# TensorE's program as a loop of four-row steps, and x in front of W: a LoRA linear layer on one core

## The chip, the core and the metric

The kernel runs on one core of a Trainium2 chip. The core has five engines that run side by side, each with a program of its own: TensorE (PE in the profile, with its weight loads as PEld), VectorE (DVE), ScalarE (ACT), GpSimd (POOL) and SyncE (SP, which here only issues transfers). Sixteen DMA engines move data between the chip's main memory and the on-chip memory SBUF, which has 128 partitions. TensorE writes its results to another memory, PSUM, and VectorE and ScalarE take them out of there. Engines wait for one another by semaphores.

The metric is the device time of one execution in microseconds (us); lower is better.

## What is computed

```python
# x (16, 2048, 256), W (256, 256), lora_A (256, 16), lora_B (16, 256), lora_E (16,), scale = 1.0
x_flat = x.reshape(-1, 256)                       # 32768 rows
y = x_flat @ W
lora_out = ((x_flat @ lora_A) * lora_E) @ lora_B
return (y + scale * lora_out).reshape(16, 2048, 256)
```

All inputs and the output are float32. x and the output have 33.55 MB each.

## The kernel before

The small matrices are folded first: `weff = W + scale * (lora_A * lora_E) @ lora_B`, once, in bf16 (lines 88 to 105: a cast, two transposes, a scaling, two matmuls and an addition). After that the whole work is `x_flat @ weff`.

The 32768 rows of x are cut into nine chunks (`PLAN`): 16 rows a partition, then seven times 32, then 16 again, times 128 partitions. A chunk is one load of 2 or 4 MB (`load`, line 66) into one of six slots of SBUF, and one store of the same size (`store`, line 70) out of the same slot, since the result is written over x in place. All loads and stores, and W ahead of them (line 73), are issued by SP and stand in one queue. SP issues W, then the loads of the first four chunks (`LEAD`); after that, whenever a chunk is done, its store and then the load of the chunk four places on. A load into a slot that was used before waits until the store out of it has landed. ScalarE issues the loads of lora_A, lora_B and lora_E.

A chunk is worked off in groups of two rows a partition (`CG`). For a group TensorE makes four transposes of 128x128 (two rows, two halves of the 256 columns) straight from the f32 data of x, into PSUM (`transposed`, line 113). VectorE casts the 128x512 result to bf16 and puts it in SBUF (line 119). TensorE multiplies the four pieces with weff, two summed into each of two rows (line 131). ScalarE copies the 128x512 result from PSUM over x (line 139).

The order of the work is that of the code. In TensorE's program the transposes of group n+1 stand in front of the products of group n, so that it has work while VectorE casts. At the end of a chunk, the products of the chunk's last group therefore stand behind the first transposes of the next chunk, and so behind that chunk's landing. Everything is written out: there is no loop on any engine, and TensorE's program has some 2,070 instructions, 16 for each of the 128 groups and a few for the small matrices.

Of the kernel before, what the change touches and what calls it, by code (L numbers as in the profile page):

```python
# [1 line left out]

# [5 lines left out]

PLAN = [16] + [32] * 7 + [16]

ROWS, SLOTS = 32, 6

LEAD = 4
CG = 2


@with_exitstack
def kernel(  # L20
    ctx: ExitStack,
    tc: tile.TileContext,
    x: bass.AP,
    W: bass.AP,
    lora_A: bass.AP,
    lora_B: bass.AP,
    lora_E: bass.AP,
    scale: bass.AP,
    out: bass.AP,
):  # L30
    nc = tc.nc
    P = 128
    FP32 = mybir.dt.float32
    BF16 = mybir.dt.bfloat16

    x_flat = x.flatten_outer_dims()
    out_flat = out.flatten_outer_dims()
    N, K = x_flat.shape
    M = out_flat.shape[1]
    R = lora_B.shape[0]  # L40
    KC = K // P
    assert K == M and sum(PLAN) * P == N

    const = ctx.enter_context(tc.tile_pool(name="const", bufs=1))
    slots = ctx.enter_context(tc.tile_pool(name="slots", bufs=SLOTS))
    xTpool = ctx.enter_context(tc.tile_pool(name="xTpool", bufs=4))
    ps_setup = ctx.enter_context(tc.tile_pool(name="ps_setup", bufs=1, space=bass.MemoryType.PSUM))
    ps_xT = ctx.enter_context(tc.tile_pool(name="ps_xT", bufs=3, space=bass.MemoryType.PSUM))
    ps_y = ctx.enter_context(tc.tile_pool(name="ps_y", bufs=3, space=bass.MemoryType.PSUM))


    ctx.enter_context(tc.manual_schedule())

    starts = [sum(PLAN[:i]) * P for i in range(len(PLAN))]

    def rows_of(flat, i):
        b, r0 = PLAN[i], starts[i]
        return flat[r0:r0 + b * P, :].rearrange("(p b) k -> p b k", b=b)

    held = []

    def load(i):
        t = slots.tile([P, ROWS, K], FP32, name="xy")
        nc.sync.dma_start(out=t[:, :PLAN[i], :], in_=rows_of(x_flat, i))  # L66
        held.append(t)

    def store(i):
        nc.sync.dma_start(out=rows_of(out_flat, i), in_=held[i][:, :PLAN[i], :])  # L70

    w_sb = const.tile([P, KC, M], FP32)
    nc.sync.dma_start(out=w_sb, in_=W.rearrange("(c p) m -> p c m", p=P))  # L73
    a_sb = const.tile([P, KC, R], FP32)
    nc.scalar.dma_start(out=a_sb, in_=lora_A.rearrange("(c p) r -> p c r", p=P))
    b_sb = const.tile([R, M], FP32)
    nc.scalar.dma_start(out=b_sb, in_=lora_B)
    e_sb = const.tile([R, 1], FP32)
    nc.scalar.dma_start(out=e_sb, in_=lora_E[:, None])

    for i in range(LEAD):
        load(i)

    ident = const.tile([P, P], FP32)
    make_identity(nc, ident)

    b_bf = const.tile([R, M], BF16)
    nc.vector.tensor_copy(out=b_bf, in_=b_sb)  # L88
    ps_at = ps_setup.tile([R, KC, P], FP32, name="ps_at")
    for c in range(KC):  # L90
        nc.tensor.transpose(ps_at[:, c, :], a_sb[:, c, :], ident)  # L91
    ate = const.tile([R, KC, P], BF16)
    nc.vector.tensor_scalar(  # L93
        out=ate,
        in0=ps_at,
        scalar1=e_sb,
        scalar2=float(scale),
        op0=mybir.AluOpType.mult,
        op1=mybir.AluOpType.mult,
    )  # L100
    ps_aeb = ps_setup.tile([P, KC, M], FP32, name="ps_aeb")
    for c in range(KC):
        nc.tensor.matmul(ps_aeb[:, c, :], ate[:, c, :], b_bf, start=True, stop=True)  # L103
    weff = const.tile([P, KC, M], BF16)
    nc.vector.tensor_add(out=weff, in0=w_sb, in1=ps_aeb)  # L105

    groups = [(i, g) for i, b in enumerate(PLAN) for g in range(b // CG)]

    def transposed(i, g):
        psum_xt = ps_xT.tile([P, CG, KC, P], FP32, name="psum_xt")  # L110
        for j in range(CG):
            for c in range(KC):
                nc.tensor.transpose(  # L113
                    psum_xt[:, j, c, :],
                    held[i][:, g * CG + j, c * P:(c + 1) * P],
                    ident,
                )
        xt = xTpool.tile([P, CG, KC, P], BF16, name="xt")
        nc.vector.tensor_copy(out=xt, in_=psum_xt)  # L119
        return xt  # L120


    ready = transposed(*groups[0])
    for n, (i, g) in enumerate(groups):
        xt = ready
        if n + 1 < len(groups):
            ready = transposed(*groups[n + 1])
        psum_y = ps_y.tile([P, CG, M], FP32, name="psum_y")
        for j in range(CG):
            for c in range(KC):  # L130
                nc.tensor.matmul(  # L131
                    psum_y[:, j, :],
                    xt[:, j, c, :],
                    weff[:, c, :],
                    start=(c == 0),
                    stop=(c == KC - 1),
                )

        nc.scalar.copy(out=held[i][:, g * CG:(g + 1) * CG, :], in_=psum_y)  # L139
        if (g + 1) * CG == PLAN[i]:  # L140
            store(i)
            if i + LEAD < len(PLAN):
                load(i + LEAD)


# [1 line left out]
_INS = ['x', 'W', 'lora_A', 'lora_B', 'lora_E', 'scale']  # L147
_OUTS = [((16, 2048, 256), 'float32')]

_NUMBERS = {'scale': 1.0}  # L150


# [26 lines left out]
```

## Time and profile before

| | us |
|---|---|
| median of three runs | 166.19 (165.45, 166.19, 166.29) |
| the profiled execution | 166.25 |
| its span, first to last instruction | 164.4 |
| PE busy | 123.3 (75% of the span) |
| DVE busy | 90.0 (55%) |
| ACT busy | 76.3 (46%) |
| POOL busy | 0.7 (0%) |
| DMA, data of x, W and out (queue q1) | 96.2% of 16 engines |

The page divides the span into 40 slices of 4.1 us and gives for each, in tenths, the share of time in which an engine was busy; for the DMA engines it is the mean over the sixteen, and GB/s is what they moved. The part on queues gives packets, MB and the share of sixteen engines' time. A row of the groups of instructions names the line, the engine, the operation, what it writes and reads with shapes, how often; then busy time and the mean of one in ns; then the idle time of the engine in front of it, and what ended it. The chain that ended last is followed back from the end of the program: at each step to what released it. SPq is SP's queue of issues. PEclk, the clock that TensorE was granted, is full for most of the span, with some slower stretches (one near 96 us), and half after the last matmul.

The transposes start at 9.68 us, when the first chunk has landed, and the last copy of ScalarE ends at 138.7. TensorE waited for loads of x four times, 6.0 us in all.

### The profile page before, as it was taken

The page shows a single profiled execution, that of the slowest core. Times are in us where ns is not written, and L with a number is a line of the kernel's source. Part 1 is how long each engine was busy: PE and PEld are TensorE (multiplying, and loading weights), DVE is VectorE, ACT ScalarE, POOL GpSimd, SP SyncE. Part 2 cuts the span into 40 slices and gives each one's busy share as a digit, 9 for nine tenths or more (in the row PEclk, how much of TensorE's full clock was granted, in tenths as well). Part 3 has the DMA queues.
Part 4 walks back from the last instruction along what each step waited for, and adds up shares of the span by engine and source line. Part 5 has one row for each costly group of instructions (what it writes and reads, how often), then busy time and mean ns, then how long its engine had stood idle before and what let it go on. Part 6 is the DMA issues. An engine that isn't in the chain of part 4 may idle for free.

```text
span 164.4 us, 2548 instructions
## 1 busy us (share of the span) xinstructions
PE 123.3 (75%) x1028; PEld 102.9 (63%) x1028; DVE 90.0 (55%) x131; ACT 76.3 (46%) x129; POOL 0.7 (0%) x6
## 2 busy tenths in 40 slices
PE   0179899999999999999999689992999995000000
PEld 0058788888888888888888478881888783000000
DVE  0065677777777777777777536771777673000000
ACT  0034566666666666666666525662566565000000
POOL 1000000000000000000000000000000000000000
PEclk9999999999999999999999978999999999655555
DMA  5999999998999999999999999999999999999991
GB/s 141 429 482 407 415 478 395 454 415 343 437 462 407 421 446 431 435 431 423 439 419 439 423 423 443 409 439 447 423 391 466 415 443 423 423 454 415 415 391 56
DMA packets 3211, 67.56 MB, mean 411 GB/s; under 512 B 624, under 2 KB 896, under 8 KB 896
## 3 DMA queue, kind: packets, MB, share of 16 engines
q1 hardware_dynamic: 2864, 67.37, 96.2%
q8 instruction: 8, 0.13, 0.3%
q10 hardware_dynamic: 336, 0.03, 0.2%
q14 instruction: 3, 0.02, 0.0%
HBM read 33.85 MB, written 33.55 MB: 410 GB/s over the span
## 4 chain that ended last, share of the span: by engine, by line
DMA 59%; PE 23%; ACT 1%; SPq 1%; DVE 0%; issue 0%
DMA xy<-in_x_dram 38%; DMA out_dram<-xy 21%; PE psum_y L131 12%; PE psum_xt L113 11%; ACT xy L139 1%; DVE xt L119 0%; SPq L66 0%; SPq L73 0%
## 5 line engine op out<-in xcount | busy, mean ns | idle before, releaser
L119 DVE CAST xt<-psum_xt 128x512 bf16<-128x512 f32 x128 | 88.5, 691 | 38.6 <-PE psum_xt L113 38.6
L139 ACT COPY xy<-psum_y 128x512 f32<-128x512 f32 x128 | 75.0, 586 | 52.7 <-PE psum_y L131 52.7
L113 PE MATMUL psum_xt<-ident,xy 128*128 128x128 f32 x512 | 79.2, 279 | 6.1 <-DMA xy<-in_x_dram 6.0
L131 PE MATMUL psum_y<-weff,xt 128*128 128x256 bf16 x512 | 79.3, 278 | 0.3 <-DVE xt L119 0.3
L113 PEld LDWEIGHTS psum_xt<-ident,xy 128*128 128x128 f32 x512 | 61.9, 144 | 9.2 <-issue 5.7
L131 PEld LDWEIGHTS <-xt 128*128 128x128 bf16 x512 | 41.1, 99 | 16.8 <-DVE xt L119 0.9
L139 ACT ACT_TABLE_LOAD x1 | 1.3, 1283 | 9.7 <-DMA xy<-in_x_dram 9.7
L103 PE MATMUL ps_aeb<-b_bf,ate 16*128 16x256 bf16 x2 | 0.6, 402 | 4.4 <-DVE ate L93 4.4
L91 PE MATMUL ps_at<-ident,a_sb 128*16 128x128 f32 x2 | 0.6, 396 | 4.0 <-DMA a_sb<-in_lora_A_dram 4.0
L88 DVE CAST b_bf<-b_sb 16x256 bf16<-16x256 f32 x1 | 0.3, 281 | 6.0 <-DMA b_sb<-in_lora_B_dram 6.0
L103 PEld LDWEIGHTS <-ate 16*128 16x128 bf16 x2 | 0.1, 102 | 4.9 <-DVE ate L93 4.9
L91 PEld LDWEIGHTS ps_at<-ident,a_sb 128*16 128x16 f32 x2 | 0.1, 88 | 4.0 <-issue 4.0
L93 DVE TENSOR_SCALAR ate<-ps_at,e_sb 16x256 bf16<-16x256 f32 x1 | 0.5, 472 | 2.2 <-DMA e_sb<-in_lora_E_dram 2.2
L105 DVE TENSOR_TENSOR weff<-w_sb,ps_aeb 128x512 bf16<-128x512 f32 x1 | 0.7, 689 | 0.7 <-PE ps_aeb L103 0.7
masks.py:199 POOL TENSOR_SCALAR_AFFINE_SELECT ident<-ident 128x128 f32<-128x128 f32 x1 | 0.3, 292 | 0.1
masks.py:197 POOL MEMSET ident<- 128x128 f32 x1 | 0.2, 204 | 0.3 <-POOLq L160 0.3
L160 POOL MEMSET const-bfloat16-1.0<- 128x1 bf16 x1 | 0.1, 101 | 0.0
L160 POOL MEMSET const-uint8-127<- 128x1 uint8 x1 | 0.1, 101 | 0.0
L160 POOL MEMSET const-float32-0.0<- 128x1 f32 x1 | 0.1, 98 | 0.2 <-issue 0.2
L160 POOL MEMSET const-float32-1.0<- 128x1 f32 x1 | 0.1, 98 | 0.0
## 6 DMA issues: line engine op xcount, KB each, us to landing
xy<-in_x_dram SPq DMA_DIRECT2D x7, 4096.0 KB, 38.0
out_dram<-xy SPq DMA_DIRECT2D x7, 4096.0 KB, 34.2
xy<-in_x_dram SPq DMA_DIRECT2D x2, 2048.0 KB, 26.6
out_dram<-xy SPq DMA_DIRECT2D x2, 2048.0 KB, 24.5
w_sb<-in_W_dram SPq DMA_DIRECT2D x1, 256.0 KB, 3.0
a_sb<-in_lora_A_dram ACTq DMA_DIRECT2D x1, 16.0 KB, 3.2
b_sb<-in_lora_B_dram ACTq DMA_DIRECT2D x1, 16.0 KB, 4.7
e_sb<-in_lora_E_dram ACTq DMA_DIRECT2D x1, 0.1 KB, 6.6
```

The source lines that it names most:

```text
L88: nc.vector.tensor_copy(out=b_bf, in_=b_sb)
L91: nc.tensor.transpose(ps_at[:, c, :], a_sb[:, c, :], ident)
L93: nc.vector.tensor_scalar(out=ate, in0=ps_at, scalar1=e_sb, scalar2=float(scale), op0=mybir.AluOpType.mult, op1=mybir.AluOpType.mult,)
L103: nc.tensor.matmul(ps_aeb[:, c, :], ate[:, c, :], b_bf, start=True, stop=True)
L105: nc.vector.tensor_add(out=weff, in0=w_sb, in1=ps_aeb)
L113: nc.tensor.transpose(psum_xt[:, j, c, :], held[i][:, g * CG + j, c * P:(c + 1) * P], ident,)
L119: nc.vector.tensor_copy(out=xt, in_=psum_xt)
L131: nc.tensor.matmul(psum_y[:, j, :], xt[:, j, c, :], weff[:, c, :], start=(c == 0), stop=(c == KC - 1),)
L139: nc.scalar.copy(out=held[i][:, g * CG:(g + 1) * CG, :], in_=psum_y)
L160: nc = _bacc.Bacc("TRN2", target_bir_lowering=False, num_devices=1)
```

## The change

The kernel is written anew with semaphores of its own, inside one critical section in which each engine's program is written out by hand. The chunks, the slots, the lead of four loads and the folding of the small matrices stay. What differs:

- SP issues the load of the first chunk, then W, then the three other loads. Afterwards the order is that of before: wait for a chunk, store, load (with the wait for the slot's old store in front of the load).
- A step has four rows a partition instead of two (`Q`). VectorE first casts the step's x from SBUF to a bf16 buffer (`round_step`, 128x1024); there are two such buffers, used in turn. TensorE transposes from there with a bf16 identity, eight transposes a step into bf16 PSUM. VectorE casts 128x1024 from PSUM to one of two `xt` buffers. Eight products go to one of two `ps_y`, and ScalarE copies 128x1024 over x.
- VectorE's order is: cast of x for step k+1, then the copy out of PSUM for step k. weff, which needs W, stands in front of the first cast of x.
- Since the buffers of TensorE are the same every second step, its program is a loop of 31 passes of two steps (transposes 1, products 0, transposes 0, products 1), with the first transposes ahead of it and the last step and a half behind it. In the loop it can't wait for growing counts, so each wait takes one off its semaphore (`take`). Per step it takes from the cast of x, from the copy out of PSUM, and from ScalarE's copy.
- ScalarE drains after the last copy of a chunk and then tells SP.

TensorE's program shrinks to 32 matmuls inside the loop and 36 outside. VectorE executes 128 casts as before, 64 of each kind, each of 1024 elements a partition; ScalarE 64 copies of 1024 elements instead of 128 of 512.

```diff
-    for i in range(LEAD):
-        load(i)
...
-    def transposed(i, g):
-        psum_xt = ps_xT.tile([P, CG, KC, P], FP32, name="psum_xt")
...
-        nc.vector.tensor_copy(out=xt, in_=psum_xt)
...
+    xb = [sbuf(f"xb{s}", [P, Q, K], BF16) for s in range(2)]
+    xt = [sbuf(f"xt{s}", [P, Q, KC, P], BF16) for s in range(2)]
...
+    ps_xt = [psum(f"ps_xt{s}", [P, Q, KC, P], BF16) for s in range(2)]
+    ps_y = [psum(f"ps_y{s}", [P, Q, M], FP32) for s in range(2)]
...
+    with tc.tile_critical(sync_engine=mybir.EngineType.SP, no_gpsimd_drain=True):
...
+        def load(i):
+            sp.dma_start(out=xy[i % SLOTS][:, :PLAN[i], :], in_=rows_of(x_flat, i)).then_inc(s_in[i], 16)
+
+        for i in range(LEAD):
+            load(i)
+            if i == 0:
+                sp.dma_start(out=w_sb[:], in_=W.rearrange("(c p) m -> p c m", p=P)).then_inc(s_w, 16)
+        for i in range(CHUNKS):
+            sp.wait_ge(s_rdy, i + 1)
+            sp.dma_start(out=rows_of(out_flat, i), in_=xy[i % SLOTS][:, :PLAN[i], :]).then_inc(s_out[i], 16)
+            if i + LEAD < CHUNKS:
+                if i + LEAD >= SLOTS:
+                    sp.wait_ge(s_out[i + LEAD - SLOTS], 16)
+                load(i + LEAD)
+        for i in range(CHUNKS):
+            sp.wait_ge(s_out[i], 16)
...
+        dve.wait_ge(s_w, 16)
+        dve.wait_ge(s_lpe, 2)
+        dve.tensor_add(out=weff[:], in0=w_sb[:], in1=ps_aeb[:]).then_inc(s_lora, 1)
+
+        def round_step(k):
+            i, r = steps[k]
+            if r == 0:
+                dve.wait_ge(s_in[i], 16)
+            if k >= 2:
+                dve.wait_ge(s_t, k - 1)
+            dve.tensor_copy(out=xb[k % 2][:], in_=xy[i % SLOTS][:, r:r + Q, :]).then_inc(s_xb, 1)
+
+        round_step(0)
+        for k in range(n):
+            if k + 1 < n:
+                round_step(k + 1)
+            dve.wait_ge(s_t, k + 1)
+            if k >= 2:
+                dve.wait_ge(s_p, k - 1)
+            dve.tensor_copy(out=xt[k % 2][:], in_=ps_xt[k % 2][:]).then_inc(s_xt, 1)
...
+        for k, (i, r) in enumerate(steps):
+            act.wait_ge(s_p, k + 1)
+            act.copy(out=xy[i % SLOTS][:, r:r + Q, :], in_=ps_y[k % 2][:]).then_inc(s_y, 1)
+            if r + Q == PLAN[i]:
+                act.drain().then_inc(s_rdy, 1)
...
+        def take(s):
+            pe.wait_ge(s, 1).then_inc(s, -1)
+
+        def transposes(k):
+            take(s_xb)
+            for j in range(Q):
+                for c in range(KC):
+                    t = pe.transpose(ps_xt[k % 2][:, j, c, :], xb[k % 2][:, j, c * P:(c + 1) * P], ident_bf[:])
+            t.then_inc(s_t, 1)
+
+        def products(k):
+            take(s_xt)
+            take(s_y)
+            for j in range(Q):
+                for c in range(KC):
+                    m = pe.matmul(
+                        ps_y[k % 2][:, j, :], xt[k % 2][:, j, c, :], weff[:, c, :],
+                        start=(c == 0), stop=(c == KC - 1),
+                    )
+            m.then_inc(s_p, 1)
...
+        transposes(0)
+        pe.wait_ge(s_lora, 4)
+        with pe.Fori(0, n // 2 - 1):
+            transposes(1)
+            products(0)
+            transposes(0)
+            products(1)
+        transposes(1)
+        products(0)
+        products(1)
```

## The prediction

> **What bounds the kernel now.** I read the row of DMA engines and the queues first, then the two ends of the stream, then SP's issues and the chain, and last the groups of instructions.
>
> ```profile
> DMA  5999999998999999999999999999999999999991
> GB/s 141 429 482 407 415 478 395 454 415 343 437 462 407 421 446 431 435 431 423 439 419 439 423 423 443 409 439 447 423 391 466 415 443 423 423 454 415 415 391 56
> ...
> q1 hardware_dynamic: 2864, 67.37, 96.2%
> q8 instruction: 8, 0.13, 0.3%
> ```
>
> The sixteen DMA engines are full from the second slice to the last but one. Reads and writes of x and out are 33.55 MB each, and the change alters neither. q8 is DMA work that is no data: 8 packets of 16 KB of code. In the DMA answers for four short windows (25:27, 40:42, 54:57, 69:71) one such packet takes 2.0 to 3.3% of sixteen engines, 0.93 to 1.06 us of one engine, and they come 14.7 us apart.
>
> The stream's ends, by windows (width, busy time of five engines, clock, DMA share, GB/s):
>
> ```profile
> 2.00:3.00 1.00, 0.00 (x0) 0.00 (x0) 0.00 (x0) 0.00 (x0) 0.00 (x0) 1.00 1.01 289
> 3.00:4.00 1.00, 0.00 (x0) 0.00 (x1) 0.00 (x0) 0.00 (x0) 0.00 (x0) 1.00 1.05 259
> 140.00:150.00 10.00, 0.00 (x0) 0.00 (x0) 0.00 (x0) 0.00 (x0) 0.00 (x0) 0.53 1.00 433
> 160.00:161.00 1.00, 0.00 (x0) 0.00 (x0) 0.00 (x0) 0.00 (x0) 0.00 (x0) 0.50 0.46 197
> 161.00:162.00 1.00, 0.00 (x0) 0.00 (x0) 0.00 (x0) 0.00 (x0) 0.00 (x0) 0.50 0.12 49
> 162.00:163.00 1.00, 0.00 (x0) 0.00 (x0) 0.00 (x0) 0.00 (x0) 0.00 (x0) 0.50 0.04 16
> ```
>
> The first 2 us of data, W and the head of x, run below the stream's pace. After 160 the engines run dry one after another: the mean engine is done at about 160.6 and the last at about 163, so the end is one late engine's, 2.5 us behind the mean. From 140 on nothing computes and the rate is 433 GB/s; in the window from 50 to 160 it was 429. Compute and stream do not slow each other visibly.
>
> SP's timeline, the table of DMA issues, and pieces of the chain (start, us):
>
> ```profile
> 138.71 0.33 SPq L70 DMA_DIRECT2D out_dram<-xy  x1
> ...
> out_dram<-xy SPq DMA_DIRECT2D x2, 2048.0 KB, 24.5
> ...
> 50.54 34.17 DMA out_dram<-xy
> 84.77 44.76 DMA xy<-in_x_dram
> 129.66 0.63 PE psum_xt L113 x4
> ```
>
> The last store is issued at 138.71 and lands some 24.5 us later, though its own 2.1 MB take 4.8 us at 433 GB/s. It stood about 19 us in a full queue. The chain's PE share (23%) is therefore no bound: compute has slack. What that slack allows I worked out with SP's order (store i waits for chunk i, load i+4 behind it): store 7 and store 8 need 9.7 + 4.8 us of stream, so chunk 7 must be done near 146. The 56 steps of four rows from the landing of chunk 1 (19.4) to there may last (146 - 19.4) / 56 = 2.26 us each. I take 2.2. Now such a step lasts 1.83 us (two groups, 0.44 + 0.44 or 0.52 each in the chain).
>
> ```profile
> L119 DVE CAST xt<-psum_xt 128x512 bf16<-128x512 f32 x128 | 88.5, 691 | 38.6 <-PE psum_xt L113 38.6
> L139 ACT COPY xy<-psum_y 128x512 f32<-128x512 f32 x128 | 75.0, 586 | 52.7 <-PE psum_y L131 52.7
> ...
> L88 DVE CAST b_bf<-b_sb 16x256 bf16<-16x256 f32 x1 | 0.3, 281 | 6.0 <-DMA b_sb<-in_lora_B_dram 6.0
> L93 DVE TENSOR_SCALAR ate<-ps_at,e_sb 16x256 bf16<-16x256 f32 x1 | 0.5, 472 | 2.2 <-DMA e_sb<-in_lora_E_dram 2.2
> ...
> SPq L174 <- PEq L174: 0.6, 2, 0.4
> ```
>
> **The change part by part.** The sum is made against the profiled execution, 166.25 us: a span of 164.4 and 1.85 around it. The median of the runs is 166.19, so the two are one.
>
> *DVE.* It gains a cast of x (SBUF to bf16, 128x1024) beside the cast out of PSUM, now 128x1024 bf16. Cast of x: at most 4 x 281 = 1.12 us (the fixed part paid four times); at least the 0.69 of a 512-element cast, since 256 elements from SBUF in 281 ns is far below 472 from PSUM, so about half a ns an element. It is nearest to L88: 0.75. PSUM cast: at most 2 x 691 = 1.38, at least 0.69 if 16-bit data go twice as fast; L119 and L93 differ by 219 ns for 256 elements, so 691 + 2 x 219 = 1.13. Sum 1.88, and 0.12 for two waits: 2.0 us a step (bounds 1.4 to 2.6). DVE becomes the slowest engine, under the allowed 2.2. Price: 0, hidden by the 19 us of queue ahead of the last store; if this cover goes (2.6), it is a rival below.
>
> *PE.* Eight products stay at 0.88 to 1.04. Eight transposes in bf16 cost at most the 0.87 of the f32 ones, perhaps half. Three takes and half a branch a step, at the 0.05 of the chain's issue gaps, add 0.2: 1.5 to 2.1. Below DVE. The takes queue transposes behind the cast of x and products behind xt and ACT; two buffers each give a ring (PSUM cast, products, transposes, two hops) of 1.13 + 0.96 + 0.87 + 0.2 = 3.2 us for two steps, also below 4. *ACT*: 64 copies, each at most 2 x 586 = 1.17. Hidden.
>
> *Start.* DVE's weff now waits for W behind the first chunk, and the first cast of x is behind weff: 0.69 + 0.75 + the transposes put the first product some 1.5 us later. At a chunk's first step DVE waits for the landing, with the last step's PSUM cast, its products, ACT's copy and SP's store behind it. PE had this same order (the next group's transposes first), and the queue covers both. Price 0. W behind x on SP moves equal bytes; its 256 KB of 1 KB rows took about 1 us at 289 GB/s and would take 0.6 in a running stream: 0 to -0.4, I take -0.2, since x's own first packets then meet the slow start.
>
> *Code.* A group on PE is 16 instructions (8 weight loads, 8 matmuls) and lasts 0.917 us, so 14.7 us is 16 groups, 256 instructions, one packet. The new program has 32 matmuls in the loop and about 36 outside it: some 150 instructions, below one packet. All 8 packets go: 7.8 us of engine time, 0.49 us of the mean engine. The end belongs to one late engine: between 0 (none of the packets was its own) and -2.5 (all lateness was theirs); one packet's 0.97 is the row, and I take -0.8. [...]
>
> *Entry and exit.* The critical section adds a NoOp and a branch on SP ahead of the first issue, 0.05 each and one hop: +0.15 (0 to 0.7, the row of the opening barrier). Behind the last landing it adds a round through all engines and about eight SP instructions: two rounds are 0.6 in the waits (L174), so 0.3, and 8 x 0.05 = 0.4, of which half overlaps: +0.5 (0.2 to 1.0).
>
> Sum: 166.25 - 0.8 - 0.2 + 0.15 + 0.5 = 165.9; the lateness of one engine is drawn anew each run (165.45 to 166.29 shown) and has one cause fewer, for which I take another 0.2 off: 165.7.
>
> **The rivals.** *A, the late engine's lag was the code.* The full -2.5, -0.4 for W and small overheads of 0.3: 163.7. For it: one engine ends 2.5 us behind. Against: the four packets I looked at cannot be told to lie on one engine, and the shares after 160 fall in steps, several engines being late. Halfway, -1.5 in all, gives 164.7.
>
> *B, DVE takes over.* At the upper bounds a step is 1.12 + 1.38 + 0.1 = 2.6 us: 19.4 + 60 x 2.6 = 175.4 for the last copy, +1.5 start, +4.8 store, +4 landing and end: about 186. It decides from 2.26 us a step. For it: rows twice as long add up there. Against: 281 ns for 256 elements.
>
> *C, the loop fetches its code again.* If each of 31 passes brought a packet, PE would stand for a small DMA in a full stream: 3.2 to 6.6 us from issue to landing (the loads of lora_A and lora_E), 1.6 to 3.3 a step on PE's 1.7: 3.3 to 5.0, and 19.4 + 60 x 3.3 + 9 = 226 or more. It decides from 0.5 us a step. Against: the body is some 72 instructions, within one packet of 256. [...]
>
> *D, the overheads win.* Nothing gained from code or W, the upper prices at both ends (+0.7, +1.0): 167.9.
>
> **How the numbers follow.** Half a per cent, 0.83 us, is about what a measurement of this kernel can tell from no change. The forecast (stream-bound, 165.4 to 167.0) has 0.43; A with its halfway case 0.36; B 0.08, C 0.03, D 0.10. Faster is A: 0.36; same 0.43; slower B, C and D: 0.21. The range reaches from A's 163.7 to D's 167.9, leaves out B and C and a little at the lower end; the likeliest case's own range is 165.0 to 166.6.
>
> **What would show it.** Right: no q8 packets inside the span; DMA shares of 9 in the same slices; casts of x near 0.75 and PSUM casts at 0.7 to 1.2 us; the last store still some 15 us or more in the queue; its end less ragged after 160. Wrong: SP waiting for ACT while the DMA row has holes (B), a long idle of PE at each pass and 16 KB packets by the dozen (C), or more than 1.5 us between the last landing and the span's end (D).

## The result: half a per cent slower

| | before | after |
|---|---|---|
| median of the runs, us | 166.13 (19 runs, 165.45 to 166.64) | 166.97 (19 runs, 166.32 to 167.45) |
| ratio, with its 95% interval | | 1.0054 (1.0043 to 1.0066) |
| profiled execution, us | 166.25 | 167.31 |
| its span, us | 164.4 | 165.5 |
| PE, DVE, ACT busy, us | 123.3, 90.0, 76.3 | 96.4, 83.9, 66.1 |

The forecast was 165.7 and leaned to faster; the kernel became slower by 0.84 us. The time is inside the range of 163.7 to 167.9, the direction is the wrong one. The largest single chance, 0.43, stood on 165.4 to 167.0, half a per cent either way; 166.97 is at its slow edge. All three computing engines work less than before, and TensorE's code (q8 below) has gone from the DMA queues, and yet the end is later.

I read the page of the changed kernel in the same order as that of before: the row of DMA engines and the queues first.

```profile
DMA  4999899998999999999999999999999999999950
GB/s 127 399 441 499 380 499 388 412 475 360 481 420 412 459 396 467 412 443 428 396 483 396 451 428 414 443 412 475 396 412 447 410 467 404 459 412 436 404 238 16
...
q1 hardware_dynamic: 2864, 67.37, 95.3%
q10 hardware_dynamic: 336, 0.03, 0.2%
q14 instruction: 3, 0.02, 0.0%
```

The stream still has no hole. The row q8 is missing: TensorE fetched no code inside the span, so the 8 packets of 16 KB are gone and no pass of the loop brought new ones. In the last but one slice the share falls from 9 tenths to 5, and the rate from 391 to 238 GB/s: most DMA engines are done earlier.

Then both ends of the stream, from the windows of the changed kernel (width, busy time of five engines, clock, DMA share, GB/s), with the long middle ahead of them:

```profile
20.00:140.00 120.00, 88.93 (x968) 79.24 (x968) 77.20 (x121) 61.66 (x62) 0.00 (x0) 0.89 1.00 429
...
2.00:3.00 1.00, 0.00 (x0) 0.00 (x0) 0.00 (x0) 0.63 (x1) 0.00 (x0) 1.00 0.97 180
3.00:4.00 1.00, 0.00 (x0) 0.00 (x0) 0.00 (x0) 0.66 (x1) 0.00 (x0) 1.00 0.72 296
160.00:161.00 1.00, 0.00 (x0) 0.00 (x0) 0.00 (x0) 0.00 (x0) 0.00 (x0) 0.50 0.19 82
161.00:162.00 1.00, 0.00 (x0) 0.00 (x0) 0.00 (x0) 0.00 (x0) 0.00 (x0) 0.50 0.15 66
162.00:163.00 1.00, 0.00 (x0) 0.00 (x0) 0.00 (x0) 0.00 (x0) 0.00 (x0) 0.50 0.08 33
163.00:164.00 1.00, 0.00 (x0) 0.00 (x0) 0.00 (x0) 0.00 (x0) 0.00 (x0) 0.50 0.00 0
```

The middle is a little faster: the same window of before has 427 GB/s, and 2 GB/s over 120 us are 0.24 MB, some 0.56 us of stream. From 160 to 161 three of sixteen engines are still busy (0.19), where it was 0.46 before. But one or two go on after 162 (0.08, where it was 0.04): 33 GB/s are two 16 KB packets a microsecond. The trace says when each of the sixteen DMA engines was done with its part of the last store:

```
last store, us:  first   median   mean     last but one   last     end of span   behind the last
before           159.85  161.34   161.15   162.30         163.44   164.40        0.95
after            159.47  159.73   160.32   162.94         164.02   165.52        1.50
difference       -0.38   -1.61    -0.83    +0.64          +0.58    +1.13         +0.55
```

This is the case in one table. The middle engine is done 1.6 us earlier and the mean 0.8, as much as I had forecast for the end; the last one is 0.6 later, and behind it stand 0.55 more of the program's end. Two engines end 3.2 and 4.3 us behind the median one, and the end waits for them. (These times are landings, read from the semaphore updates; the packets themselves end some 0.4 us earlier.)

Computing has become lighter and is not on the path. SP's timeline gives the issue of the last store (start, duration), and the table of DMA issues its way to landing (KB, median us):

```profile
140.21 0.33 SPq L107 DMA_DIRECT2D out_dram<-xy  x1
```

```profile
out_dram<-xy SPq DMA_DIRECT2D x2, 2048.0 KB, 22.5
```

It is issued 1.5 us later than before, and still stands in a full queue. The row's 22.5 us are the median of the two stores of 2 MB; from the issue of the last one to its last landing at 164.02 are 23.8 us, of which its own 2.1 MB take 4.8. The chain that ended last holds 2.1 us of one step, the one that releases this store, and no other computing:

```profile
138.07 1.05 PE ps_y L182 x8
139.12 0.02 issue
139.14 1.01 ACT xy L161
```

The groups of the changed kernel show what a step of four rows costs each engine:

```profile
L161 ACT COPY xy<-ps_y 128x1024 f32<-128x1024 f32 x64 | 64.8, 1013 | 71.7 <-PE ps_y L182 71.7
...
L144 DVE CAST xb<-xy 128x1024 bf16<-128x1024 f32 x64 | 43.7, 684 | 34.3 <-DMA xy<-in_x_dram 34.3
...
L153 DVE COPY xt<-ps_xt 128x1024 bf16<-128x1024 bf16 x64 | 44.2, 691 | 9.3 <-PE ps_xt L174 8.1
```

DVE needs 684 + 691 ns, ACT 1013, so neither DVE (rival B) nor the loop (rival C) has become the bound of a step for which 2.26 us were allowed. DVE waits 34.3 us for loads, which shows that it is the stream that sets the pace.

### The profile page after: what moved, and what is told of

Same layout as the page of the kernel before. It is cut to its first block, busy times and chain, and to the rows that moved or that the text cites. A ratio compares the mean times of both kernels' runs of the same rounds, so it can differ in the third digit from the quotient of the medians.

```text
span 165.5 us, 2679 instructions
## 1 busy us (share of the span) xinstructions
PE 96.4 (58%) x1028; PEld 84.6 (51%) x1028; DVE 83.9 (51%) x132; ACT 66.1 (40%) x65; POOL 0.7 (0%) x6
## 5 line engine op out<-in xcount | busy, mean ns | idle before, releaser
L161 ACT COPY xy<-ps_y 128x1024 f32<-128x1024 f32 x64 | 64.8, 1013 | 71.7 <-PE ps_y L182 71.7
L182 PE MATMUL ps_y<-weff,xt 128*128 128x256 bf16 x512 | 71.5, 286 | 0.8 <-PEq L168 0.3
L174 PE MATMUL ps_xt<-ident_bf,xb 128*128 128x128 bf16 x512 | 43.0, 233 | 32.1 <-PEq L168 32.1
L144 DVE CAST xb<-xy 128x1024 bf16<-128x1024 f32 x64 | 43.7, 684 | 34.3 <-DMA xy<-in_x_dram 34.3
L174 PEld LDWEIGHTS ps_xt<-ident_bf,xb 128*128 128x128 bf16 x512 | 37.1, 105 | 36.0 <-issue 34.1
L182 PEld LDWEIGHTS ps_y<-weff,xt 128*128 128x128 bf16 x512 | 49.6, 102 | 7.9 <-issue 1.7
L153 DVE COPY xt<-ps_xt 128x1024 bf16<-128x1024 bf16 x64 | 44.2, 691 | 9.3 <-PE ps_xt L174 8.1
## 6 DMA issues: line engine op xcount, KB each, us to landing
out_dram<-xy SPq DMA_DIRECT2D x2, 2048.0 KB, 22.5
```

The lines of the kernel that those rows point to most:

```text
L144: dve.tensor_copy(out=xb[k % 2][:], in_=xy[i % SLOTS][:, r:r + Q, :]).then_inc(s_xb, 1)
L153: dve.tensor_copy(out=xt[k % 2][:], in_=ps_xt[k % 2][:]).then_inc(s_xt, 1)
L161: act.copy(out=xy[i % SLOTS][:, r:r + Q, :], in_=ps_y[k % 2][:]).then_inc(s_y, 1)
L174: t = pe.transpose(ps_xt[k % 2][:, j, c, :], xb[k % 2][:, j, c * P:(c + 1) * P], ident_bf[:])
L182: m = pe.matmul(ps_y[k % 2][:, j, :], xt[k % 2][:, j, c, :], weff[:, c, :], start=(c == 0), stop=(c == KC - 1),)
```

## The experiments

Each kernel is a variant of the changed one, where not said otherwise. Ratios are to the kernel of before on the same chip, with 95% intervals.

### Undoing one part at a time

W ahead of x again in the changed kernel:

```diff
+        sp.dma_start(out=w_sb[:], in_=W.rearrange("(c p) m -> p c m", p=P)).then_inc(s_w, 16)
         for i in range(LEAD):
             load(i)
-            if i == 0:
-                sp.dma_start(out=w_sb[:], in_=W.rearrange("(c p) m -> p c m", p=P)).then_inc(s_w, 16)
```

> The changed kernel with W issued in front of the first load of x again, all else as changed. Theory S (the start costs): in the changed kernel the second chunk landed 0.4 us later than before and the DMA share was 0.72 and 0.89 from 3 to 5 us; with W in front the stream is full from the start again, and the time falls by 0.3 to 0.4 us, to about 166.6. Theory L (the late engine costs): the end is set by one DMA engine that falls back while the core computes, 4.3 us behind the median engine; the order at the start does not touch that, and the time stays within 0.15 us of the changed kernel's 166.97.

Measured: 167.28 us (11 runs), ratio 1.0059 (1.0040 to 1.0079). The median is 0.3 us higher, where one theory had it fall and the other had it stay; by the ratios (1.0059 against 1.0054) it is 0.1 us and not told apart from nothing. The other way round, the kernel of before with nothing changed but the order:

```diff
+    load(0)
     nc.sync.dma_start(out=w_sb[:], ...)
...
-    for i in range(LEAD):
+    for i in range(1, LEAD):
```

> The kernel before with one part alone of the change: the first load of x in front of W in SP's queue. Theory S: the loss at the start comes with it, +0.3 to +0.4 us, about 166.5. My prediction's term for W: -0.2, about 165.9. If the late engine alone decides, no difference beyond 0.15 us from 166.13.

Measured: 166.02 us (12 runs), ratio 0.9978 (0.9963 to 0.9993). By the medians x in front of W is worth 0.3 us in the first pair and 0.2 in the second (the kernel of before took 166.22 us on this chip), by the ratios 0.1 and 0.4. The sign is the forecast one, and the interval of the second pair does not reach 1; the size is not sharp. This kernel is ahead of the one of before by 0.2 per cent.

TensorE's 31 passes written out, everything else as in the changed kernel:

```diff
-        with pe.Fori(0, n // 2 - 1):
+        for _ in range(n // 2 - 1):
```

> The changed kernel with TensorE's 31 passes written out instead of the loop, same instructions and waits otherwise. Theory F (the fetches matter as I predicted): some 8 code packets of 16 KB come back in the span, the median engine ends about 0.5 us later and the late one up to 1 us later: 167.4 to 167.9. Theory L (the late engine is late for another reason, and the fetches fall on engines that have room): packets come back, the median engine ends later, and the time stays within 0.3 us of 166.97.

Measured: 166.62 us (12 runs), ratio 1.0025 (1.0010 to 1.0040). The queues of this kernel have the code again:

```profile
q8 instruction: 8, 0.13, 0.3%
```

With 8 packets of code in the stream the kernel is 0.35 us faster than without. This contradicts the sign of the prediction's largest term, and the gain is a little more than theory L allowed. The pair was run once more, side by side on one chip:

> The changed kernel once more, unaltered, on the same chip as the two variants beside it. 166.8 to 167.1 by both theories; the distance of the loop to the written-out program (0.35 us so far, from different jobs) is to be read inside one job.

> The changed kernel with the 31 passes written out once more, beside the loop on the same chip. If the loop's 0.35 us is real: 166.5 to 166.7, and its interval does not meet that of the loop. If it was a difference of jobs: within 0.15 us of the loop.

Measured: the loop 167.07 us (6 runs), ratio 1.0060 (1.0039 to 1.0081); written out 166.66 us (12 runs), ratio 1.0034 (1.0018 to 1.0050). The means of the two sets of runs differ by 0.53 us, with an interval of 0.28 to 0.79, though the two ratios' intervals overlap. So the difference has been found twice with the same sign, at 0.35 to 0.5 us. The windows at the end, first of the loop, then of the written-out program:

```profile
160.00:161.00 1.00, 0.00 (x0) 0.00 (x0) 0.00 (x0) 0.00 (x0) 0.00 (x0) 0.50 0.23 98
161.00:162.00 1.00, 0.00 (x0) 0.00 (x0) 0.00 (x0) 0.00 (x0) 0.00 (x0) 0.50 0.08 33
162.00:163.00 1.00, 0.00 (x0) 0.00 (x0) 0.00 (x0) 0.00 (x0) 0.00 (x0) 0.50 0.12 49
```

```profile
160.00:161.00 1.00, 0.00 (x0) 0.00 (x0) 0.00 (x0) 0.00 (x0) 0.00 (x0) 0.50 0.38 164
161.00:162.00 1.00, 0.00 (x0) 0.00 (x0) 0.00 (x0) 0.00 (x0) 0.00 (x0) 0.50 0.15 66
162.00:163.00 1.00, 0.00 (x0) 0.00 (x0) 0.00 (x0) 0.00 (x0) 0.00 (x0) 0.50 0.00 0
```

Written out, more engines are still busy at 160 (0.38) and none after 162; as a loop, fewer at 160 and two past 162 (0.12). By engine: median 161.12 and last 162.76 written out, median 159.66 and last 163.74 as a loop. It is the picture of before and after again, now with nothing else changed: with the code's packets the median engine is 1.5 us later at the end, and the last one is 1.0 us earlier. Early in the stream it is the other way: the last landing near 40 us is at 40.95 in the first written-out run and at 38.94 in the loop. The section on passes and packets comes back to this.

### The critical section's price

A second, nearly empty section behind the first:

```diff
+    with tc.tile_critical(sync_engine=mybir.EngineType.SP, no_gpsimd_drain=True):
+        nc.sync.sem_inc(s_y, 1)
```

> The changed kernel with a second critical section behind the first, which only adds one to a semaphore: the suspected cost of entry and exit twice. Theory O (overheads): between the last landing and the span's end lay 0.95 us before and 1.50 us in the changed kernel, and the first issue came 0.2 us later; a second section adds a whole entry and exit, 0.6 to 0.9 us: 167.6 to 167.9. If the longer end is something else (the nine waits for the stores, the landing itself), less than 0.3 us: 167.0 to 167.3.

Measured: 167.67 us (7 runs), 0.70 above the changed kernel's median; ratio 1.0070 (1.0045 to 1.0096). The ratios alone differ by only 0.3 us, and their intervals overlap. The profile is sharper: the span ends 2.21 us behind the last landing (164.19 to 166.40), with one section 1.50, with none 0.95. So a section's exit costs 0.55 to 0.7 us. Its entry is read from SP's first issue, of before (first line) and of the changed kernel (second):

```profile
0.74 0.42 SPq L73 DMA_DIRECT2D w_sb<-in_W_dram  x1
```

```profile
0.94 0.38 SPq L99 DMA_DIRECT2D xy<-in_x_dram  x1
```

The entry costs 0.20 us. Together that is 0.75 in the profiles, where 0.65 was forecast; the medians say 0.7 for a second section and the ratios 0.3.

### Where the late engine comes from

First the stream without any computing: stores go behind the landing of their load, and the programs of GpSimd, VectorE and TensorE and ScalarE's copies are gone; the output is x.

```diff
-            sp.wait_ge(s_rdy, i + 1)
+            sp.wait_ge(s_in[i], 16)
...
...
```

> The changed kernel without any computing: SP's loads and stores, W and ScalarE's three small loads in the same order, each store waiting for its own chunk's landing; so the output is x itself, and the products are left out. Theory L (computing holds one or two DMA engines back): without computing all engines end within 1 us of each other, the last landing is near 160.5 and the time near 163.5. If the late engine is late by itself (its place, its share of the memory), it ends 3 us or more behind the median engine here too, and the time stays at 166.5 to 167.

Measured: 165.64 us (8 runs), ratio 0.9958 (0.9938 to 0.9978). The changed kernel stands 1.3 us above this order of transfers with one section and nothing computed. The result lies between the two expectations: even here one engine ends 2.2 us behind the median one. How far the last engine is behind the median one, at some of the landings, from the two traces:

```
landing near, us     39    53    72    92    121   136   145   160
after                0.4   0.7   1.7   2.6   3.5   4.2   4.3   4.3
transfers only       0.5   0.7   0.8   1.3   1.5   2.2   2.2   2.2
```

The lag grows while loads and stores alternate, and stops when only stores are left. About half of it needs no computing. It grows in steps where a load gives way to a store, where single packets of 32 KB on a few engines take up to 0.8 us longer than the usual 1.213, and, with computing, also evenly: in the changed kernel some packets of stores, most of them on one engine at a time, take about 1.30 us. The next question was whose work does that.

TensorE's transposes and products left out after the first two steps (only their semaphores are kept, written out):

```diff
-        with pe.Fori(0, n // 2 - 1):
-            transposes(1)
...
+        for k in range(n - 2):
+            take(s_xb)
+            pe.sem_inc(s_t, 1)
+            take(s_xt)
+            take(s_y)
+            pe.sem_inc(s_p, 1)
```

> The changed kernel with TensorE's transposes and products left out after the first two steps; it only passes the semaphores on, while VectorE's casts and ScalarE's copies run as before. The changed kernel is 1.3 us slower than its transfers alone. If TensorE's reads or its clock hold the late DMA engine back: 165.7 to 166.0. If VectorE's or ScalarE's accesses do: 166.7 to 167.0.

ScalarE's copies left out (x is stored as it came):

```diff
-            act.copy(out=xy[i % SLOTS][:, r:r + Q, :], in_=ps_y[k % 2][:]).then_inc(s_y, 1)
+            act.sem_inc(s_y, 1)
```

> The changed kernel with ScalarE's copies left out, so that x is stored as it was loaded; ScalarE only passes the semaphores on. If ScalarE's writes into the slots that are about to be stored hold the late DMA engine back: 165.7 to 166.1. If VectorE or TensorE do it: 166.6 to 167.0.

Measured: without TensorE's work 166.58 us (12 runs), ratio 1.0012 (0.9996 to 1.0028), as the written-out program with all of it; the last engine ends at 163.85. Without ScalarE's copies 167.17 us (12 runs), ratio 1.0041 (1.0017 to 1.0066), last engine at 164.35. Neither time falls to what was expected if that engine alone were the cause. The traces say more. Five stretches up to 135 us hold stores alone (54 to 63, 73 to 82, 92.7 to 101.5, 112.3 to 120.5, 127.5 to 135 us). In them 19 packets of 32 KB take between 1.26 and 1.345 us in the changed kernel, 17 without ScalarE's copies, none without TensorE's work, and none in the transfers alone. So the even part of the lag goes with TensorE's work. But without that work the steps are larger in the profiled run (which, at 167.14 us, was the slowest of the twelve), its lag still reaches 3.8 us, and it is not shown how much of the 1.3 us this part is worth. VectorE's casts were not left out in any run. I turned to the code, and put more of it, with next to no work in it, beside the stream.

On GpSimd, 1,024 waits that are already met, four for each of a partition's 256 rows (two of the expectations below say 1,152), beside the whole changed kernel. The profile has 512 semaphore instructions for them:

```diff
+        for i, rows in enumerate(PLAN):
+            for _ in range(4 * rows):
+                pool.wait_ge(s_in[i], 16)
```

> The changed kernel, loop and all, with some 1,000 waits that are soon met added to GpSimd's program, which does nothing else by then: code packets come back into the span (GpSimd's, of 8 KB), while TensorE keeps its loop. Written-out passes were 0.35 us faster than the loop (166.62 against 166.97). If that came from the code packets, which put the sixteen DMA engines out of step, the time falls to 166.6 to 166.8. If it came from the loop itself, it stays at 166.9 to 167.1; if packets cost what my prediction said, it rises to 167.3 or more.

And on TensorE, 8 a row and 6 more, in the transfers-only kernel:

```diff
+        for i, rows in enumerate(PLAN):
+            for _ in range(8 * rows + 6):
+                pe.wait_ge(s_in[i], 16)
```

> The transfers alone (no products; the output is x, as in the run of transfers only), and a TensorE program of some 2,100 waits that are already met, so that about 8 code packets of 16 KB are fetched over the span and nothing is computed. Theory F (my prediction's term: fetches cost the end 0.5 to 1 us): 166.1 to 166.6 against 165.64 without them. Theory K (the packets fall on engines that have room, and put the sixteen out of step, which helps the late one): 165.3 to 165.6, although the mean engine ends about 0.6 us later.

Measured: GpSimd's waits cost 1.1 us by the medians and 0.9 by the ratios, 168.08 (6 runs), ratio 1.0112 (1.0087 to 1.0136), which is what was expected if packets cost what the prediction said. They bring 4 more packets of code, of 8 KB and 0.31 us each (the first line below; the changed kernel has 3), 1.2 us of one engine if all fell on the late one. TensorE's waits missed their aim: their 1,051 semaphore instructions came 0.106 us apart, TensorE itself ended last, and the time was 176.95 us (5 runs), ratio 1.0635 (1.0606 to 1.0664), which says nothing of the stream. SP's row of waits shows it (second line):

```profile
q14 instruction: 7, 0.06, 0.1%
```

```profile
SPq L94 <- PEq L94: 9.8, 1, 9.8
```

Its last landing does say something: it was at 163.57 against 162.14 without the waits. The run has 4 packets of 16 KB on q8, not the 8 that were expected, and between the landings before and after the first of them, at 84.96 us, the last engine's lag goes from 0.3 to 3.3 us. The same GpSimd waits on the transfers-only kernel end in time:

> The transfers-only kernel (nothing is computed; stores go behind the landing of their load) and on GpSimd 1,152 waits that are already met, 4 per row of a chunk, which bring 4 more code packets of 8 KB on another queue than x. Beside computing the same waits cost 1.1 us. If instructions executed beside the transfers, or their code packets, hold the late DMA engine back by themselves: 166.3 or more. If they do so only beside computing: 165.5 to 165.8, as without them (165.64).

Measured: 166.39 us (12 runs), ratio 1.0012 (0.9994 to 1.0031), 0.75 above the transfers-only kernel (by the ratios, 0.9). Only four packets of code in all, 0.31 us each, and the last engine at 162.99 instead of 162.14. So instructions beside the stream, with hardly any data of their own, make its end later, without any computing. The trace shows that a packet can do it: the last of the four, at 128.30 us, begins where a packet of the engine that ends last is done, and that engine's next packet of 32 KB takes 1.301 us instead of 1.213, 0.40 us for both. Two of the others, at 88.42 and 107.24, may stand on the same engine, but another runs in step with it there, and the trace does not tell which of the two it is. How much is left for the waits being executed is not shown.

### The loop's 0.35 us: passes or missing packets?

Three passes over ten written-out pairs of steps, and one pair behind:

```diff
-        with pe.Fori(0, n // 2 - 1):
...
+        with pe.Fori(0, 3):
+            passes(10)
+        passes(1)
```

> [...] If packets matter as in the written-out form, 166.6; if the number of passes matters, the same; if the loop form as such costs, 167.0.

Measured: 166.60 us (12 runs), ratio 1.0023 (1.0008 to 1.0038), with 3 packets of code in all, where I had assumed that every pass would fetch its own. It is a loop, and as fast as the written-out program. Five passes over six pairs, in the same manner (`pe.Fori(0, 5)`, `passes(6)`):

> The changed kernel, with TensorE's loop as 5 passes over six written-out pairs of steps and one pair behind it, instead of 31 passes over one pair. Three passes over ten pairs measured 166.60 us with 3 code packets of 16 KB, 31 passes 166.97 with none. Six pairs are about 430 instructions, so I expect one packet of 16 KB or none. If it is the missing packets that cost the 0.35 us: 166.8 to 167.0, as after. If it is the 31 passes (their branches and what TensorE does at them): 166.6 to 166.7, as the written-out program.

Measured: 166.68 us (12 runs), ratio 1.0037 (1.0022 to 1.0052), with 2 packets, one more than was expected at most. By what was expected this speaks for the passes as the cause. So the jumps were multiplied, with a control:

```diff
             products(1)
+            with pe.Fori(0, 4):
+                pe.wait_ge(s_w, 16)
```

> The changed kernel with a second loop inside TensorE's pass: four rounds of one wait that is already met. That makes 124 more taken branches (155 in place of 31) and 124 more met waits; no code packet is added. With 8, 3, 2 and 0 code packets and 0, 3, 5 and 31 passes the program so far took 166.66, 166.60, 166.68 and 167.07 us. If the passes cost (0.4 us per 31): 167.0 + 4 x 0.4 = 168.6 us, and well above the run beside it, which has the waits alone. If it was the missing packets: as the run beside it, 167.0 to 167.3.

> The changed kernel with four waits that are already met written out at the end of each pass of TensorE's loop: 124 more instructions, the same 31 taken branches. 1,152 such waits on GpSimd cost 1.1 us, so 124 cost about 0.1: 167.0 to 167.2 by both theories. It is the control for the run with the inner loop.

Measured: with the inner loop 166.95 us (8 runs), ratio 1.0053 (1.0034 to 1.0072); with the four waits written out 166.82 us (12 runs), ratio 1.0038 (1.0018 to 1.0058). 124 more jumps cost 0.1 us, within the uncertainty, where 1.6 was due if 31 cost 0.4. A cost of jumps is not the cause.

What is left is the packets. The rows of q8, first of the ten pairs, then of the six:

```profile
q8 instruction: 3, 0.05, 0.1%
```

```profile
q8 instruction: 2, 0.03, 0.1%
```

And the packets beside the times:

| | code packets on q8 | passes | us | ratio to before | last engine in the profile, us |
|---|---|---|---|---|---|
| written out | 8 | 0 | 166.62 and 166.66 | 1.0025 and 1.0034 | 163.04 and 162.76 |
| ten pairs | 3 | 3 | 166.60 | 1.0023 | 163.25 |
| six pairs | 2 | 5 | 166.68 | 1.0037 | 163.50 |
| after | 0 | 31 | 166.97 and 167.07 | 1.0054 and 1.0060 | 164.02 and 163.74 |
| waits in the pass | 0 | 31 | 166.82 | 1.0038 | 164.18 |
| inner loop | 0 | 155 | 166.95 | 1.0053 | 163.50 |

Of these six programs those with some packets are at 166.6 to 166.7, those with none at 166.8 to 167.1. The border is not sharp: by the ratios the waits in the pass stand where the six pairs do.

The landings of the same profiles show where the loss arises. How far the last engine is behind the median one, in us:

```
landing near, us             19    29    39    73    92    111   126   136   160
before, 8 packets            0.7   1.3   2.0   1.8   2.5   2.2   2.3   2.0   2.1
before, x first, 8           0.3   1.4   1.9   2.9   2.8   3.1   2.6   2.6   2.6
written out, 8 packets       0.5   1.8   2.4   2.3   2.9   2.6   2.3   1.9   1.9
written out again, 8         0.4   1.4   2.0   2.1   2.8   2.4   2.0   1.6   1.6
ten pairs, 3                 0.2   1.6   2.5   2.7   3.0   3.4   3.4   3.4   3.4
six pairs, 2                 0.2   1.4   2.1   2.8   3.3   3.3   3.7   3.7   3.8
after, none                  0.2   0.2   0.4   1.7   2.6   3.1   3.8   4.2   4.3
inner loop, none             0.2   0.2   0.3   1.5   2.1   2.4   2.8   3.4   3.5
```

In every row with packets the first one comes between 25.4 and 28.3 us, and at the landing behind it the last engine is 1.3 to 1.8 us behind; without packets it is 0.2. So a packet does put an engine behind, as the prediction had it. From 39 to 136 us the lag then grows by 3 to 4 us without packets, by 1.6 with two, by 0.9 with three, and with eight by 0.7 or not at all. (With eight, part of that is the median engine, which is later itself: 161.1 at the end against 159.7.) The loop's loss is the difference of the two: without packets the later growth is larger than the early lag with them. Each row is one execution. Why the lag grows less where packets come is not shown.

### Splitting the last store

The question is which engine is late. For it the last store goes in two transfers, of 120 and of 8 partitions, on the kernel of before with x first and on the changed kernel.

```diff
+        ends = (0, 120, P) if i == len(PLAN) - 1 else (0, P)
+        for p0, p1 in zip(ends, ends[1:]):
+            nc.sync.dma_start(out=rows_of(out_flat, i)[p0:p1], in_=held[i][p0:p1, :PLAN[i], :])
```

> The kernel before with x in front of W (166.02 us), and its last store of 2 MB cut into partitions 0 to 119 and 120 to 127. [...]

> The changed kernel with its last store cut in the same way. Its late engine is some 1.1 to 1.7 us behind the next. [...]

Measured: 167.91 us (6 runs), ratio 1.0110 (1.0066 to 1.0154), and 170.84 us (6 runs), ratio 1.0280 (1.0251 to 1.0309). Both are worse, by 1.9 and 3.9 us. That a transfer of 120 partitions would spare the late engine was my assumption, and no run shows it. In the changed kernel with the split one engine was still busy alone (0.04, one 16 KB packet a microsecond) at 166:

```profile
161.00:162.00 1.00, 0.00 (x0) 0.00 (x0) 0.00 (x0) 0.00 (x0) 0.00 (x0) 0.50 0.35 131
163.00:164.00 1.00, 0.00 (x0) 0.00 (x0) 0.00 (x0) 0.00 (x0) 0.00 (x0) 0.50 0.12 49
166.00:167.00 1.00, 0.00 (x0) 0.00 (x0) 0.00 (x0) 0.00 (x0) 0.00 (x0) 0.50 0.04 16
```

That engine worked off nine packets of 16 KB one behind the other, from 161.7 to 167.2, the last four of them alone. The queue has 7 packets more than without the split. Many of the transfer's packets of 16 KB took 0.9 to 1.9 us in the changed kernel, and up to 2.7 in the other, where 0.61 is usual. Which engine it is the trace does not tell, and as a means the split costs time here.

## Why the prediction was wrong

**Bound.** Right: the stream bounds both kernels, and one late engine sets the end. That computing and the stream do not slow each other, as I read from 433 and 429 GB/s, does not hold for this end: with nothing computed the changed kernel's transfers are done 1.3 us sooner. After 140 us nothing but the stream is left, and the chain holds no computing but the 2.1 us of the step that releases the last store.

**DVE, PE, ACT.** Right that they are hidden. The cast of x was put at 0.75 and took 0.684 us. The PSUM cast was put at 1.13 and took 0.691, at the lower end of my bounds: 1024 bf16 elements a partition go out of PSUM in the 691 ns that 512 of f32 take in L119 of before. On PE, near 101 us, a step's transposes start 0.45 us ahead of the products, and these 0.87 us ahead of the next transposes, 1.32 a step where 1.5 to 2.1 were forecast. ACT's copy took 1.013, below the bound of 1.17.

**Start, W.** Right in sign: 0.2 forecast, 0.2 to 0.3 by the medians of both experiments, 0.1 and 0.4 by their ratios.

**Entry and exit.** Right: +0.65 forecast, 0.75 in the profiles (0.20 and 0.55).

**Code.** This is the step that failed. The prediction let the end gain 0.8 from the missing packets, and a further 0.2 since lateness would have "one cause fewer". Measured, the loop is 0.35 to 0.5 us slower than the written-out program. The first half of the mechanism was right: all 8 packets went, the stream's middle rose from 427 to 429 GB/s, and the mean engine was done 0.83 earlier. There was even ground for a credit: in the landings of before the last engine is 0.7 us behind ahead of the first two packets, and 1.3 and then 2.0 after them. What failed is the step from there to the end. It took the lag for a sum from which one packet's worth can be subtracted, with nothing in its place. In the changed kernel the last engine has a lag of only 0.4 us at 39 us, and then falls almost 4 us further behind by 136, where before it fell no further. The term's upper bound, 0, had no ground either: I had excluded a loss without a reason that a row gave.

**The sum.** With the measured terms: 166.13 - 0.25 (W) + 0.75 (section) + 0 (the new step, written out) = 166.63, beside 166.62 and 166.66 of the written-out program; + 0.35 for the loop = 166.98, and 166.97 was measured. The 0 for the new step is what this sum leaves, no run has the step without the section, and the other terms are known to 0.1 or 0.2 us only.

**Rivals.** A (the lag was the code) is refuted as a forecast: without code packets the lag is 4.3 us, and about half of that is there without computing, though the packets did make the early lag of before. B is closed by DVE's 1.38 us a step. C is closed by the missing q8 row. D, the overheads win, is nearest: nothing gained from the code, and the section's price to pay. But its terms were others, since W did gain and the section cost no more than the sum had, and a loss from the missing packets is in none of the rivals. Its sign, more than 1.5 us between the last landing and the span's end, came out at 1.50. That the time lies inside the range is owed to D's upper prices, which did not come, and so to luck; the likeliest case's own range ended at 166.6. With the code at nothing, and no 0.2 for lateness, the sum's own terms give 166.25 - 0.2 + 0.65 = 166.7.

## What to carry to other kernels

Where sixteen DMA engines bound a kernel, read when the last of them is done, not only their mean. Work that is taken off the engines counts only if the last one ends earlier for it; here the mean engine was done 0.83 us earlier and the last one 0.58 later. Even packets that do put the last engine behind are no credit as they stand: without them another lag can grow, as it did here, from 0.4 us at 39 us to 4.2 at 136. Follow the last engine's lag from landing to landing before crediting a saving to the end, and leave room for a loss. The section with semaphores of its own cost about 0.75 us once here, so it needs something on the path to pay for it; the one part here that paid, x in front of W, needed two lines.

## What the runs showed of the hardware

- With nothing computed the last of the sixteen DMA engines falls from 0.5 to 2.2 us behind the median between 39 and 136 us, while loads and stores alternate, and beside the changed kernel from 0.4 to 4.2; once only stores are left it falls no further.
- Some packets of stores take 1.26 to 1.345 us instead of 1.213 while TensorE works: 19 in five stretches of the changed kernel, none with TensorE's work left out, none with nothing computed.
- 1,024 waits that are met, on GpSimd, make the end of the stream 0.75 us later without computing and 0.9 to 1.1 with it. Of their four code packets of 0.31 us at least one stands on the engine that ends last.
- A loop of TensorE with 155 jumps instead of 31 costs nothing that can be measured (166.95 to 166.82). Three passes over ten pairs, some 720 instructions long, fetched only 3 packets of code in all, at 25.95, 40.80 and 87.10 us, none of them between the first jump back at 43.5 and the second at 84.4.
